# A two-layer attention and expert network on one core: a nineteenth weight slot in the second layer, and two more experts of the first layer added up in DRAM

## The chip, the core and the metric

The kernel runs on one core of a Trainium2 chip. The metric is the device time of one execution in microseconds (us), lower is better; a kernel is run several times and the median counts.

## What is computed

The reference is two layers over 512 latent tokens and 256 context tokens of width 1024, all in fp32. Each layer has three groups of mixing heads, an output projection, and then an expert-choice feed-forward: every one of 16 experts picks its own tokens (64 latent ones, and in the first layer 32 context ones), runs them through a gated two-matrix layer of width 512 and a down matrix, weighs the rows by the gate value and adds them back to their tokens. Cut to the part that matters here:

```python
def ec_ffn(h, router_w, w_gate, w_up, w_down):
    cap = EC_CAPACITY_FACTOR * n_tok // N_EXPERTS
    aff = jax.nn.softmax((h @ router_w).astype(jnp.float32), axis=-1)
    top_aff, idx = lax.top_k(jnp.swapaxes(aff, 1, 2), cap)
    xg = jax.vmap(lambda hb, ib: hb[ib])(h, idx)
    hid = jax.nn.silu(einsum(xg, w_gate)) * einsum(xg, w_up)
    y = einsum(hid, w_down) * top_aff[..., None]
    return zeros.at[idx].add(y)
...
xl = xl + g2 * ec_ffn(...)          # latent tokens, both layers
xc = xc + cg2 * ec_ffn(...)         # context tokens, first layer only
```

The result is the RMS-normed latent stream after the second layer.

## The kernel before, in words

`layer(li, ada)` is run for both layers; `upd` is true in the first one only. The last stage of a layer is a loop over the experts, `for e in range(NE + 1)`, and all of the change lies there and in the buffers that feed it. TensorE (PE) executes in the order in which the program is written (`manual_schedule`); the order on the other engines and on the DMA queues is set by the framework's scheduler, under the waits that tiles impose.

**Weights.** An expert has six halves of 1 MB: two of the gate matrix, two of the up matrix (`load_gu`), two of the down matrix (`load_d`). Each goes into a slot of 8 KB a partition. The slots come from several pools that `slot()` takes in a cycle: three of `ringa`, three or nine of `ringb` (`RING_B`), and `RING_D` more, opened once the output projection's operands are gone. In the second layer that makes 3 + 9 + 6 = 18 slots. The loads are issued on SP's queue (two in the second layer on POOL's), and each waits until PE has read the former content of its slot, and also, as SP's loads share eight semaphores in turn, until the load eight before it has landed. SP handles its list strictly in order.

**One turn of the loop.** PE does the gate and up matmuls of expert e (`gate_up`: 64 rows, in the first layer also 32 context rows), the down matmuls of expert e - 1 for the latent rows (`down`, called by `finish`), the transposes of the gathered rows of expert e + 1 (`columns`, evacuated into `xgT` by ACT at L1013 and DVE at L1015), the transposes of the hidden rows (`hid_t`, evacuated into `hTe` by ACT at L1053), and some pieces of `combine`. In the first layer `hid_t` belongs to expert e itself and the down matmuls of the 32 context rows come at the end of the turn; in the second layer rows are gathered for two experts at once.

**Adding the rows back.** There are two ways. For experts below `in_dram` (12 in the first layer, 0 in the second) DVE scales the down result into a tile `ya` of 96 rows (L1073) and POOL adds its rows to `acc`, a copy of the stream in DRAM, with an indirect DMA that accumulates (L1076). For the others DVE scales it into `yt` (L1082), ACT and DVE split it into a high and a low part `yp` (L1086, L1087; the context rows go to `y1`, L1095, and later to `yc`), POOL builds a one-hot matrix `pl`, and PE multiplies the two (`combine`, tile `cb`) so that DVE can add the product to the stream `xl` or `xc` in SBUF (L1120). `combine` covers two experts at a time for the latent rows: 16 matmuls into eight pieces, each of which one DVE addition takes up. `todo` holds the pieces; `fill` emits some of them a turn and the rest after the loop. Before the first such addition the stream is read back from `acc`: six DMAs on POOL's queue (L1194), in turn NE - 2.

What follows after the loop in the first layer is the second layer's norm of `xl` (ACT, L307), which needs the last additions.

## Time and profile before

| | |
|---|---|
| runs of the kernel | 1432.83 us median (1432.7, 1432.83, 1435.84) |
| the profiled execution's own time | 1436.76 us |
| its span, first to last instruction | 1435.0 us |
| mean granted clock of TensorE | 0.958 |
| PE busy | 1284.1 us (89%) |
| DVE, ACT, POOL busy | 710.2, 513.5, 216.7 us |
| moved by DMA | 321.16 MB |
| experts of the first layer | about 520 to 840 us of the span |
| experts of the second layer | about 1190 to 1420 us |

A busy PE is not PE at its peak, since matmuls are pipelined and their ends are modelled. So the argument goes by stretches of the span: who waits for whom there, what the granted clock is, and how busy the DMA engines are.

### The profile page before, as it was taken

Reading aid. Unit: us, or ns where it says so; the run is one execution under the profiler, and the core shown is the slowest. Engines: PE = TensorE matmul, PEld = TensorE weight load, DVE = VectorE, ACT = ScalarE, POOL = GpSimd, SP = SyncE. Lnnn points to the kernel's source line nnn. Section 1 sums busy time; section 2 is a strip of 40 time slices with the busy share of each in tenths; the row PEclk is TensorE's granted clock in tenths of the full one; section 3 lists DMA queues with packets and bytes.
Section 4 is the critical chain, followed back from the end, with each engine's and each line's share of the span. In section 5 each row is a group of like instructions: output and inputs, shape, how many; then the busy total and the mean of one; then the engine's idle time right before and its main releaser. Section 6 shows DMA issues by size and latency. Waiting matters only on the chain. (4 is left out here: it accounts for less than half of the span.)

```text
span 1435.0 us, 21605 instructions
## 1 busy us (share of the span) xinstructions
PE 1284.1 (89%) x8598; PEld 811.0 (57%) x8598; DVE 710.2 (49%) x1564; ACT 513.5 (36%) x1093; POOL 216.7 (15%) x252
## 2 busy tenths in 40 slices
PE   3989989989999959999999959998999968999986
PEld 0768866656678833444443438876778754343332
DVE  1545266566653453333333484847876352333435
ACT  2523145455543322222222143436666232232222
POOL 1111001313120230111110120101232011111201
PEclk9989999999999979999999989999999988999998
DMA  9523416535661389999999610210016447999993
GB/s 359 190 88 118 161 40 235 184 132 195 246 235 54 138 313 363 374 375 376 374 374 389 243 57 32 72 63 1 2 35 258 163 190 303 419 420 419 420 421 124
DMA packets 54084, 321.16 MB, mean 224 GB/s; under 512 B 8528, under 2 KB 8656, under 8 KB 20448
## 3 DMA queue, kind: packets, MB, share of 16 engines
q1 hardware_dynamic: 45664, 286.75, 51.2%
q0 software_dynamic: 8320, 33.03, 7.2%
q8 instruction: 68, 1.11, 0.3%
q14 instruction: 32, 0.26, 0.1%
HBM read 304.52 MB, written 15.24 MB: 223 GB/s over the span
## 5 line engine op out<-in xcount | busy, mean ns | idle before, releaser
L59 PE MATMUL mm<-slot,xgT 128*32 128x256 f32 (+1 forms) x2048 | 289.1, 492 | 5.6 <-DMA slot<-in_exp_w_up_dram 3.9
L59 PE MATMUL mm<-hT,w 128*128 128x512 f32 (+1 forms) x1176 | 228.9, 354 | 3.3 <-POOL w L135 2.0
L59 PEld LDWEIGHTS mm<-hT,w 128*128 128x128 f32 x1176 | 191.4, 191 | 37.1 <-POOL w L135 2.4
L59 PEld LDWEIGHTS mm<-slot,xgT 128*32 128x32 f32 (+1 forms) x2048 | 104.2, 125 | 178.7 <-issue 144.7
L59 PE MATMUL mm<-slot,hTe 128*32 128x256 f32 (+1 forms) x1024 | 150.2, 503 | 0.8 <-ACT hTe L1053 0.8
L1044 DVE TENSOR_TENSOR gh<-mm,gh 64x512 f32<-64x512 f32 (+1 forms) x48 | 29.0, 604 | 226.7 <-ACT gh L1043 225.5
L1043 ACT ACTIVATE gh<-mm 64x512 f32<-64x512 f32 (+1 forms) x48 | 24.9, 519 | 243.1 <-PE mm L59 243.1
L59 PE MATMUL mm<-wo,mixb 128*128 128x512 f32 x360 | 99.1, 411 | 2.3 <-DVE mixb L135 1.3
L1013 ACT ACTIVATE xgT<-tp,modT,a 128x64 f32<-128x64 f32 (+1 forms) x192 | 68.9, 426 | 84.3 <-PE tp L1009 80.9
L59 PEld LDWEIGHTS mm<-slot,hTe 128*32 128x32 f32 (+1 forms) x1024 | 51.1, 126 | 81.5 <-issue 69.1
L689 ACT COPY pt<-tp 128x512 f32<-128x512 f32 (+1 forms) x120 | 64.9, 542 | 82.6 <-PE tp L686 81.4
L686 PE MATMUL tp<-ident,p 128*128 128x128 f32 x552 | 87.4, 284 | 5.5 <-ACT pt L689 2.3
L676 POOL TENSOR_SCALAR p<-p,sm 128x768 f32<-128x768 f32 (+1 forms) x30 | 58.5, 1950 | 124.4 <-DVE sm L675 116.1
L686 PEld LDWEIGHTS tp<-ident,p 128*128 128x128 f32 x552 | 61.5, 142 | 27.8 <-issue 18.7
L59 PE MATMUL ada<-slot,sT 128*32 128x512 f32 x384 | 54.6, 689 | 23.6 <-DMA slot<-in_ada_w_dram 23.6
L59 PEld LDWEIGHTS mm<-wo,mixb 128*128 128x128 f32 x360 | 65.3, 192 | 16.9 <-DVE mixb L135 2.2
L59 PE MATMUL sc<-kt,qh 96*128 96x512 f32 (+1 forms) x324 | 69.7, 348 | 0.0
L134 ACT CAST w<-slot 128x1024 fp32r<-128x1024 f32 x30 | 31.4, 1046 | 100.1 <-PE mm L59 73.8
L59 PE MATMUL sc<-kst,qst 128*128 128x256 f32 (+1 forms) x288 | 48.1, 298 | 20.6 <-DVE mx L673 12.9
L665 DVE TENSOR_REDUCE mx<-sc 128x1 f32<-128x768 f32 (+1 forms) x60 | 51.0, 851 | 26.9 <-PE sc L59 25.9
L996 POOL DMA_INDIRECT xg<-tabx,gidx x24 | 23.2, 968 | 252.4 <-PE tp L1051 149.4
L59 PEld LDWEIGHTS sc<-kt,qh 96*128 96x128 f32 x324 | 52.6, 190 | 10.0 <-issue 3.4
(246 smaller groups left out, 1794.6 us busy)
## 6 DMA issues: line engine op xcount, KB each, us to landing
slot<-in_exp_w_gate_dram SPq DMA_DIRECT2D x62, 1024.0 KB
slot<-in_exp_w_up_dram SPq DMA_DIRECT2D x62, 1024.0 KB
slot<-in_exp_w_down_dram SPq DMA_DIRECT2D x62, 1024.0 KB
slot<-in_ada_w_dram SPq DMA_DIRECT2D x48, 1024.0 KB
slot<-in_win_dram SPq DMA_DIRECT2D x14, 1024.0 KB
slot<-in_wo_dram SPq DMA_DIRECT2D x8, 1024.0 KB
tabx<-xn POOLq DMA_DIRECT2D x10, 512.0 KB, 3.0
xt<-in_x_dram SPq DMA_DIRECT2D x4, 512.0 KB
```

The lines of the kernel that those rows point to most:

```text
L59: PE.matmul(o, l, r, start=start, stop=stop, skip_group_check=True)
L134: (hi or V.tensor_copy)(out[0], x)
L665: V.tensor_reduce(mx, sc[:, :n], axis=AX.X, op=OP.max, negate=True)
L676: (G if s and self.kind == "mla" else V).tensor_scalar(p[:, :n], p[:, :n], sm, None, op0=OP.mult)
L686: PE.transpose(ps[:, b * 128:(b + 1) * 128], p[:, (b0 + b) * 128:(b0 + b + 1) * 128], ident)
L689: S.copy(o, ps[:, :n * 128])
L996: G.indirect_dma_start(out=xg, out_offset=None, in_=tabx[li], in_offset=bass.IndirectOffsetOnAxis(ap=gidx[:ng, c:c + 1], axis=0))
L1013: S.activation(xgT[:, k0 + k, :n], ps[:, k * ng:k * ng + n], AF.Identity, bias=b[:, 0:1], scale=s[:, 0:1])
L1043: S.activation(gh[64:128, :n], ps[0:64, :n], AF.Silu)
L1044: V.tensor_tensor(gh[0:64, :n], ps[64:128, :n], gh[64:128, :n], op=OP.mult)
```

## The change

`RING_D` gives the second layer seven slots instead of six there, 19 in all. The room is made in the pool `ex`: one `xgT` instead of two in both layers, and in the second layer one `gh` and one `hTe` instead of two. In the first layer `in_dram` rises from 12 to 14: experts 12 and 13 (they are counted from 0) are added up in `acc` as well, and only 14 and 15 go through `combine`. With that the read-back moves from the middle of turn 14 to its end, behind the accumulating DMA of expert 13, and the context tile `y1` holds rows of two experts only, so that `split` takes its upper 64 partitions.

```diff
--- before.py
+++ after.py
@@ -35,7 +35,7 @@
 RING_0 = 6
 RING_A = 3
 RING_B = (3, 9)
-RING_D = (8, 6)
+RING_D = (8, 7)
 AHEAD = 2
 PB = 5
 PTB = 3
@@ -1002,7 +1002,7 @@
                 xgTs[e] = xgTs[e - 1]
                 return
             xg = xgs[e]
-            xgT = xgTs[e] = ex.tile([128, KD, ng], F32, name="xgT")
+            xgT = xgTs[e] = ex.tile([128, KD, ng], F32, name="xgT", bufs=1)
             for k0 in range(0, KD, 4):
                 ps = ps_tp()
                 for k in range(4):
@@ -1039,7 +1039,7 @@
                     for q in range(4):
                         mm(ps[32 * q:32 * q + 32, :n], xgT[:, k, CAPL:],
                            wgu[q // 2][k][:, (q % 2) * n:(q % 2 + 1) * n], k == 0, k == KD - 1)
-            gh = hids[e, r] = ex.tile([128, FF], F32, name="gh")
+            gh = hids[e, r] = ex.tile([128, FF], F32, name="gh", bufs=2 if upd else 1)
             S.activation(gh[64:128, :n], ps[0:64, :n], AF.Silu)
             V.tensor_tensor(gh[0:64, :n], ps[64:128, :n], gh[64:128, :n], op=OP.mult)
 
@@ -1049,7 +1049,7 @@
             ps = ps_tp()
             for c in range(n // 128):
                 PE.transpose(ps[:, c * 64:c * 64 + 64], hid[0:64, c * 128:(c + 1) * 128], ident[:64, :64])
-            hT = hTs[e, r] = ex.tile([128, n // 2], F32, name=f"hTe{r}")
+            hT = hTs[e, r] = ex.tile([128, n // 2], F32, name=f"hTe{r}", bufs=2 if upd else 1)
             S.copy(hT, ps[:, :n // 2])
 
         Y = {}
@@ -1089,7 +1089,7 @@
                 return
 
             i = e % np_
-            if i == 0:
+            if e == in_dram:
                 Y[r] = ex.tile([128, D], F32, name=f"y{r}", bufs=1)
             for q in range(np_):
                 V.scalar_tensor_tensor(Y[r][i * rows:(i + 1) * rows, q * n:(q + 1) * n], ps[rows * q:rows * (q + 1), :n],
@@ -1105,9 +1105,9 @@
 
         def split(g):
 
-            o = [ex.tile([128, D], F32R, name=f"yc{i}", bufs=1) for i in range(2)]
-            parts(Y[1], o, S.copy)
-            pl = places(1, g)
+            o = [ex.tile([128, D], F32R, name=f"yc{i}", bufs=1)[64:128] for i in range(2)]
+            parts(Y[1][64:128], o, S.copy)
+            pl = places(1, g)[64:128]
             return [(pl, [y[:, hf * 512:(hf + 1) * 512] for hf in range(2)]) for y in o]
 
         def combine(r, terms):
@@ -1126,7 +1126,7 @@
         rs = range(len(streams))
         todo, pair = [], []
 
-        in_dram = 12 if upd else 0
+        in_dram = NE - 2 if upd else 0
 
         def finish(e, r):
             down(e, r)
@@ -1148,7 +1148,7 @@
                 x = X["xl"][tb]
                 for hf in range(2):
                     steps[2 * tb + hf]()
-                    j = p.tile([128, 512], F32, name="gh")
+                    j = p.tile([128, 512], F32, name="gh", bufs=1)
                     S.activation(j, x[:, hf * 512:(hf + 1) * 512], AF.Square, accum_out=sq2[:, tb, hf:hf + 1])
                 sq = small.tile([128, 1], F32, name="ssq")
                 V.tensor_tensor(sq, sq2[:, tb, 0:1], sq2[:, tb, 1:2], op=OP.add)
@@ -1187,11 +1187,6 @@
                     columns(e + 1)
                 if e + 2 < NE:
                     gather(e + 2)
-                if upd and e == NE - 2:
-
-                    for i, t in enumerate(X["xl"] + X["xc"]):
-                        V.tensor_copy(t[:, 0:1], xgTs[NE - 1][:, 0, 0:1])
-                        G.dma_start(t, acc[i * 128:(i + 1) * 128, :])
                 if upd:
                     for r in reversed(rs):
                         hid_t(e, r)
@@ -1199,6 +1194,11 @@
             if e:
                 for r in rs[1:] if upd else rs:
                     finish(e - 1, r)
+            if upd and e == in_dram:
+
+                for i, t in enumerate(X["xl"] + X["xc"]):
+                    V.tensor_copy(t[:, 0:1], xgTs[NE - 1][:, 0, 0:1])
+                    G.dma_start(t, acc[i * 128:(i + 1) * 128, :])
         if upd:
             fill(len(todo))
         else:
```

PE's list loses the 16 `cb` matmuls of experts 12 and 13 and is otherwise the same. On the engines and queues that the prediction speaks of, the order moves as follows.

ACT in turn 13 of the first layer (`xgT` and `hTe` are the evacuations that PE's transposes wait for, `yp` is the split of expert 12), before:

```order
L1013 ACTIVATE xgT<-tp,modT_102,a_0_2041 128x64 x2
L1086 CAST yp<-yt 64x512 x2
L1013 ACTIVATE xgT<-tp,modT_102,a_0_2041 128x64 x2
L1053 COPY hTe_6729<-tp 128x128
L1013 ACTIVATE xgT<-tp,modT_102,a_0_2041 128x64 x2
L1053 COPY hTe_6736<-tp 128x256
L1013 ACTIVATE xgT<-tp,modT_102,a_0_2041 128x64 x2
```

and in the change:

```order
L1043 ACTIVATE gh<-mm 64x256
L1043 ACTIVATE gh<-mm 64x512
L1013 ACTIVATE xgT<-tp,modT_102,a_0_2041 128x64 x2
L1053 COPY hTe_6723<-tp 128x128
L1053 COPY hTe_6730<-tp 128x256
L1013 ACTIVATE xgT<-tp,modT_102,a_0_2041 128x64 x6
```

The two casts of `yp` are gone from between the evacuations, and `hTe` is no longer behind further pieces of `xgT`; turn 14 changes in the same way. This is also how turns 1 to 12 stand before and after.

POOL at the end of the first layer's experts, with the semaphores that each row waits for (DMASW are those of POOL's own DMAs), before:

```order
L1076 DMA acc<-ya,gidx 768x1024 [waits DMASW0_49,DVE_49]
L996 DMA xg<-tabx_88,gidx 96x1024 [waits DMASW1_49,PE_49]
L1194 DMA xl_3838<-acc 128x1024 [waits DMASW2_49,DVE_49]
L1194 DMA xl_3839<-acc 128x1024 [waits DVE_49]
L1194 DMA xl_3840<-acc 128x1024 [waits DVE_49]
L1194 DMA xl_3841<-acc 128x1024 [waits DVE_49]
L1194 DMA xc_3845<-acc 128x1024 [waits DVE_49]
L1194 DMA xc_3846<-acc 128x1024 [waits DVE_49]
L1103 TENSOR_SCALAR pl_6994<-tok,st_4662 128x512 [waits PE_49,Pool_49]
L1103 TENSOR_SCALAR pl_7069<-tok,st_4662 128x512 [waits PE_49,Pool_49]
```

and in the change:

```order
L996 DMA xg<-tabx_88,gidx 96x1024 [waits DMASW1_49,PE_49]
L1076 DMA acc<-ya,gidx 768x1024 [waits DMASW2_49,DVE_49]
L1076 DMA acc<-ya,gidx 768x1024 [waits DMASW4_49,DVE_49]
L1201 DMA xl_3838<-acc 128x1024 [waits DMASW5_49]
L1201 DMA xl_3839<-acc 128x1024
L1201 DMA xl_3840<-acc 128x1024
L1201 DMA xl_3841<-acc 128x1024
L1201 DMA xc_3845<-acc 128x1024
L1201 DMA xc_3846<-acc 128x1024 [waits DMASW3_49]
```

Two accumulating DMAs stand ahead of the read-back now, and its first DMA waits for the landing of the second of them. The one-hot matrices of experts 14 and 15 are built long before, in the place of those of 12 and 13.

SP in the second layer, the weight loads from the gate matrix of expert 12 on (each row is two halves, or as many as stand behind it), before (gate and up of 12; down of 11 and 12; gate and up of 13, of 14; down of 13; gate and up of 15; down of 14 and 15):

```order
L761 DMA slot<-in_exp_w_gate_dram 128x2048 x2
L761 DMA slot<-in_exp_w_up_dram 128x2048 x2
L769 DMA slot<-in_exp_w_down_dram 128x2048 x4
L761 DMA slot<-in_exp_w_gate_dram 128x2048 x2
L761 DMA slot<-in_exp_w_up_dram 128x2048 x2
L761 DMA slot<-in_exp_w_gate_dram 128x2048 x2
L761 DMA slot<-in_exp_w_up_dram 128x2048 x2
L769 DMA slot<-in_exp_w_down_dram 128x2048 x2
L761 DMA slot<-in_exp_w_gate_dram 128x2048 x2
L761 DMA slot<-in_exp_w_up_dram 128x2048 x2
L769 DMA slot<-in_exp_w_down_dram 128x2048 x4
```

and in the change (gate and up of 12, of 13; down of 12 and 13; gate and up of 14; one half of down of 14; gate and up of 15; the last three down halves):

```order
L761 DMA slot<-in_exp_w_gate_dram 128x2048 x2
L761 DMA slot<-in_exp_w_up_dram 128x2048 x2
L761 DMA slot<-in_exp_w_gate_dram 128x2048 x2
L761 DMA slot<-in_exp_w_up_dram 128x2048 x2
L769 DMA slot<-in_exp_w_down_dram 128x2048 x4
L761 DMA slot<-in_exp_w_gate_dram 128x2048 x2
L761 DMA slot<-in_exp_w_up_dram 128x2048 x2
L769 DMA slot<-in_exp_w_down_dram 128x2048
L761 DMA slot<-in_exp_w_gate_dram 128x2048 x2
L761 DMA slot<-in_exp_w_up_dram 128x2048 x2
L769 DMA slot<-in_exp_w_down_dram 128x2048 x3
```

Early down halves stand elsewhere in the stream now: ahead of expert 14's gate and up instead of ahead of expert 13's. And one half, of expert 3's gate matrix, has moved ahead of the point where SP first has to wait for PE to free a slot: counted from that point on SP's queue, the first half of the up matrix of expert 13 was the 63rd load and is the 60th; that of expert 14 was the 67th and is the 68th; the last load was the 78th and is the 77th.

## Rows read from the trace of the kernel before

**Rows 1.** PE in order of time, first layer, turns 12 to 14: start, length

```profile
738.49 10.76 PE L59 MATMUL mm<-slot,xgT 128*32 128x256 f32 x96
...
754.15 0.46 PE L1051 MATMUL tp<-ident,gh 64*128 64x64 f32 x4 [0.38 <-ACT hTe L1053]
754.53 1.93 PE L59 MATMUL mm<-slot,hTe 128*32 128x256 f32 x32
756.28 10.75 PE L59 MATMUL mm<-slot,xgT 128*32 128x256 f32 x96
...
773.80 0.69 PE L1051 MATMUL tp<-ident,gh 64*128 64x64 f32 x4 [2.26 <-ACT hTe L1053]
774.41 3.64 PE L59 MATMUL mm<-slot,hTe 128*32 128x256 f32 x32
```

**Rows 2.** Busy time by stretch: us, five engines (instructions), clock, DMA share, GB/s

```profile
760.00:800.00 40.00, 35.49 (x259) 14.85 (x260) 13.39 (x36) 10.49 (x28) 5.25 (x8) 0.88 0.98 378
```

**Rows 3.** PE in order of time, first layer, turn 15 and the end

```profile
799.80 10.94 PE L59 MATMUL mm<-slot,xgT 128*32 128x256 f32 x96
...
814.61 3.44 PE L59 MATMUL cb<-yp,pl 128*128 128x512 f32 x12
817.98 5.52 PE L59 MATMUL mm<-slot,hTe 128*32 128x256 f32 x48
...
830.53 5.50 PE L59 MATMUL cb<-yp,pl 128*128 128x512 f32 x15 [3.62 <-DVE yp L1087]
```

**Rows 4.** ACT in order of time there

```profile
824.42 1.26 ACT L1086 CAST yp<-yt 64x512 fp32r<-64x512 f32 x2 [9.33 <-PE cb L59]
```

**Rows 5.** DVE in order of time there, and its copies ahead of the read-back

```profile
814.22 0.75 DVE L1082 SCALAR_TENSOR_TENSOR yt<-mm,gw,g2l 128x512 f32<-128x512 f32 x1 [2.06 <-PE mm L59]
...
819.98 1.97 DVE L1095 SCALAR_TENSOR_TENSOR y<-mm,gw,g2c 32x256 f32<-32x256 f32 x4 [0.92 <-PE mm L59]
...
829.70 1.40 DVE L1087 TENSOR_TENSOR yp<-yt,yp 64x512 fp32r<-64x512 f32 x2
...
831.66 1.88 DVE L1120 TENSOR_TENSOR xl<-xl,cb 128x512 f32<-128x512 f32 x3
...
838.76 2.48 DVE L1120 TENSOR_TENSOR xc<-xc,cb 128x512 f32<-128x512 f32 x4 [0.59 <-PE cb L59]
...
L1193 DVE COPY xl<-xgT x4: 144/144/145, 794.1 to 794.5; 128x1 f32<-128x1 f32 x4
```

**Rows 6.** POOL in order of time: the accumulating DMA of expert 11

```profile
759.61 1.44 POOL L1076 DMA_INDIRECT acc<-ya,gidx  x1 [4.91 <-DVE ya L1073]
```

**Rows 7.** DMA issues by line, whole span: count, KB each, median us to landing

```profile
xl<-acc POOLq DMA_DIRECT2D x4, 512.0 KB, 7.6
...
xc<-acc POOLq DMA_DIRECT2D x2, 512.0 KB, 14.0
...
xg<-tabx,gidx POOLq DMA_INDIRECT x24, 9.3
acc<-ya,gidx POOLq DMA_INDIRECT x12, 9.8
```

**Rows 8.** PE in order of time, second layer, gate and up of experts 10, 12 to 14

```profile
1321.58 7.04 PE L59 MATMUL mm<-slot,xgT 128*64 128x512 f32 x32
...
1348.80 7.04 PE L59 MATMUL mm<-slot,xgT 128*64 128x512 f32 x32
...
1367.60 8.45 PE L59 MATMUL mm<-slot,xgT 128*64 128x512 f32 x30 [3.90 <-DMA slot<-in_exp_w_up_dram]
...
1382.85 7.04 PE L59 MATMUL mm<-slot,xgT 128*64 128x512 f32 x32
```

**Rows 9.** Busy time by stretch, second layer (columns as in rows 2)

```profile
1190.00:1205.00 15.00, 14.48 (x75) 7.78 (x75) 0.69 (x1) 4.78 (x10) 5.16 (x4) 0.90 0.55 186
1355.00:1370.00 15.00, 10.62 (x40) 3.68 (x38) 5.29 (x8) 2.20 (x4) 3.13 (x2) 0.90 1.01 420
```

**Rows 10.** The chain that ended last, its first piece: start, us, what

```profile
1189.91 4.32 DMA xg<-tabx,gidx
```

## The prediction

> **What bounds the kernel now.** I read the stretches that the change touches, not the shares over the span. In the first layer's experts a turn of PE's loop takes 17.79 us (738.49 to 756.28 [rows 1]), and within it PE waits 0.38 us for an evacuation by ACT. Turn 13 is different. Expert 12 is the first that isn't added up in DRAM; ACT makes its two `yp` casts between the evacuations, and PE waits 2.26 us for `hTe` instead of 0.38. The 32 matmuls after that wait took 3.64 us instead of 1.93: TensorE was granted its lower level, 1.2 of 2.4 GHz, after the wait, and over 760 to 800 us the mean is 0.88 [rows 1, 2]. Turn 14 repeats this, so turn 15 begins at 799.80 [rows 3], where two more turns of 17.79 us after 756.28 would have begun it at 791.86. Behind turn 15 stand the 16 `cb` matmuls of experts 12 and 13, then a wait of 3.62 us before the `cb` of 14 and 15 [rows 3]. The reason is in ACT's row: the cast of expert 14's `yp` had waited 9.33 us for PE to finish reading the `yp` of experts 12 and 13 [rows 4]. So the end of the first layer is a chain through ACT and DVE that begins with those two experts. DMA isn't late there: no row of PE in it waits for one.
>
> In the second layer PE and DMA run neck and neck. The DMA engines are full (share 1.01, 420 GB/s [rows 9]), so a half of 1.05 MB takes 2.5 us, and PE catches up with the stream once: in turn 13 it waits 3.90 us for the first up half of expert 13 and then takes 8.45 us for 30 matmuls, for which the row at full clock gives 30/32 of 7.04, or 6.60 [rows 8]; the clock's mean over 1355 to 1370 us is 0.90, its lower level again [rows 9].
>
> **The change, part by part.**
>
> *First layer, turns 13 and 14.* The `yp` casts leave ACT's list, so these turns become like turn 12, and turn 15 begins at 756.28 + 2 x 17.79 = 791.86. In turn 14 DVE's six one-column copies remain; at 0.145 us each they may hold up an evacuation, and I add all six, 0.87 [rows 5]: 792.73 instead of 799.80. (Bounds: 0 to 0.87 for the copies.) DVE's work for an expert becomes six `ya` scalings in place of `yt`, `yp` and `y1`; this is what turns 1 to 12 carry within 17.79 us.
>
> *First layer, the end.* From the start of turn 15 to the end of its transposes nothing changes: 814.61 - 799.80 = 14.81 us [rows 3]. That gives 807.54. No `cb` follows; PE does the 48 down matmuls in 5.52 us at once [rows 3]: 813.06. The `yp` of expert 14 is made beside them, since its buffers are free. Expert 15: `yt` 0.75, the first cast on ACT 0.63 (half of 1.26), then two subtractions of 0.70, which hide the second cast: 815.84; then four pieces of `y1`, 1.97: 817.81 [rows 4, 5]. There DVE's additions to `xl` begin. Before, they began at 831.66 [rows 5], and from there to the second layer the work is the same (eight additions, the context's part, the norm). **Term: -13.85 us.** In it are the two long waits, the low clock, the 16 `cb` matmuls (4.6 us at 3.44 for twelve) and the wait behind them; I don't add them again.
>
> *The read-back, now late.* The accumulating DMA of expert 11 was issued 3.33 us after turn 13 began (759.61 against 756.28 [rows 1, 6]), so that of expert 13 comes at 792.73 + 3.33 = 796.06 and lands 9.8 us later, at 805.9 [rows 7]. The six loads follow at once, some 0.56 us apart. In the trace they took 7.6 us (`xl`) and 14.0 us (`xc`), beside a full stream of weights [rows 7]. So `xl` is there at about 813.5 and the last `xc` at 808.7 + 14.0 = 822.7. They are needed at 817.8, and, as the additions to `xc` began 7.1 us after those to `xl` [rows 5], at 824.9. I cost the read-back at nothing; the cover is 4.3 and 2.2 us, and what exceeds it is paid in full. The trace of before shows no wait of this kind, since the last accumulating DMA was issued at 759.61 and the copies ahead of the read-back ran at 794.1 [rows 5, 6]. The Trainium skill, page "DMA: Bandwidth & Descriptors", section "Two DMAs through the same engine are not ordered", says that a DMA which reads what an earlier one writes is ordered by nothing but the earlier one's completion semaphore, even on one queue. By that rule the loads cannot be queued behind the accumulating DMA at 797.5 and must start at 805.9; the sum stays as it is by either, and only the chance of the first rival rises.
>
> *Two more accumulating DMAs* put 0.4 MB each into a busy stretch, about 1 us of the engines each at 420 GB/s; PE waits for no DMA there, so nothing.
>
> *One buffer for `xgT`, `gh`, `hTe`.* On PE the readers of the old content stand ahead of the transposes or matmuls whose result replaces it, or (for `gh`) directly behind, with a whole turn until it is needed: nothing. If that fails, an evacuation would be late by one group of transposes, under 1 us a turn.
>
> *Second layer, the nineteenth slot.* One half more is loaded before PE begins, so each later place in the stream is worth 2.5 us less, and the order has changed. Expert 13's first up half was the 63rd load and landed at about 1367.6; as the 60th it lands at 1360.1, before PE asks for it: that wait goes. Next is expert 14's, the 68th: 1367.6 + 5 x 2.5 = 1380.1. PE needs two turns of together 27.22 us from turn 12 on (1348.80 - 1321.58 [rows 8]) and is there at 1376.0. So it waits 4.1 us one turn later. If it then runs as slowly as before, for 8.45 - 6.60 = 1.85 us, turn 14 counts as begun at 1381.95 instead of 1382.85 [rows 8]. **Term: -0.9 us** (bounds: -2.75 without the slow start, +1 if the stream restarts less smoothly, a rounding of half a load).
>
> *Second layer, the first gather.* The extra half joins the burst of loads that ends about when the gather of the first two experts is issued: between 1190 and 1205 us the engines are at 0.55 [rows 9], and the gather took 4.32 us [rows 10]. Beside a full stream a gather takes 9.3 us [rows 7]. With 2.5 us more of load in front it lies between +0 and +5.0; only part of one half can still be ahead of it, so I take half of 2.5. **Term: +1.3 us**, on the path, as PE's first matmuls wait for it and the stream's restart waits for PE.
>
> **Sum:** -13.85 - 0.9 + 1.3 = -13.45 us. The profiled execution took 1436.76 us, 1.76 above its span of 1435.0; it would take 1423.3. The median of the runs, 1432.83, is 3.9 below that execution, and I take the difference over: **1419.4 us**.
>
> **The rivals.** *The read-back is late.* For: it has to wait for a landing that nothing made it wait for before, and its cover is 2 to 4 us. Against: the durations I used are those beside a full stream, while the last weights are in by then. It decides from a landing of the accumulating DMA at 808.1 on. With loads of twice the length, `xl` would come at 821.1 (3.3 us late) and `xc` at 836.7 (11.8 late): 1422.7 to 1431.2.
>
> *The second layer's wait goes for good and the gather isn't delayed.* Then 3.90 + 1.85 us and the small remainder vanish: 1432.83 - 13.85 - 5.75 = 1413.2. For: PE has only this one long wait there [rows 8]. Against: DMA is the fuller of the two [rows 9], and expert 14's halves are five places later.
>
> *Slower than before.* The six loads run one after the other instead of side by side, behind the wait. At 7.6 us each the last is in at 805.9 + 45.6 = 851.5, which is 26.6 us after it is needed: 1446. It decides from 5.4 us for one load on, (824.9 + 13.45 - 805.9) / 6. Against: issued 0.56 us apart, the sixth took 14.0 us, so together they needed about 2.8 us each even then.
>
> *The change doesn't do what it says:* the slot frees no earlier load, the first layer's part holds: 1420.3 or, with the gather, 1420; this lies within the forecast's range.
>
> **How the numbers follow.** Forecast (1416 to 1422.5): 0.72. Late read-back: 0.13. Second layer wins fully: 0.09. Slower: 0.03. No change, because another chain stands right behind the first layer's end: 0.03. A measurement of this kernel can tell about 0.3%, 4.3 us, from no change. Forecast, the second layer's win and most of the late read-backs are faster by more: 0.93; 0.03 for the same (the rest of the late ones, and most of no change), 0.04 slower (the slower rival, and what is left of no change). The range from 1413.5 to 1425 leaves out half of the late read-backs, a part of the second layer's win, and the last two: under 2 in 10.
>
> **What would show it.** Right: PE's waits for `hTe` in turns 13 and 14 about 0.4 us and the clock 1.00 over 760 to 800; turn 15 at about 792.7; the read-back issued near 806; the first addition to `xl` near 818, after DVE's `y1`; in the second layer no DMA wait in turn 13 and one of about 4 us in turn 14; a wait of 1 to 2 us for the first gather. Wrong: DVE's or PE's first `cb` row waiting for the `xl` load, or the layers' border less than 10 us earlier.

## The result, and the profile after

The changed kernel takes 1422.2 us (median of 8 runs, 1417.35 to 1427.99); the kernel before, run beside it, 1436.16 us (8 runs). The ratio is 0.9901, 95% interval [0.9877, 0.9925]: about 1% faster, inside the range and 2.8 us above the number given. The profiled execution of the change took 1423.59 us; the working, made against the profiled execution of before, had given 1423.3.

Cut at marks that both profiles have (starts of PE's rows), the two executions compare so:

| stretch | before, us | after, us | predicted | measured |
|---|---|---|---|---|
| start to turn 0 of the first layer's experts | 528.23 | 525.71 | 0 | -2.52 |
| turn 0 to turn 15 | 271.57 | 265.05 | -7.07 | -6.52 |
| turn 15 to the second layer's first transposes | 45.09 | 38.90 | -6.78 | -6.19 |
| from there to the transposes behind the router's choice | 343.41 | 346.34 | 0 | +2.93 |
| from there to gate and up of expert 0 | 7.25 | 7.95 | +1.3 | +0.70 |
| from there to the end | 239.44 | 237.87 | -0.9 | -1.57 |
| sum (span) | 1434.99 | 1421.81 | -13.45 | -13.18 |

The two predicted parts of the first layer are the term of 13.85, split at the start of turn 15. The rows with +2.93 and -2.52 hold only work that the change leaves alone; over the fourteen profiles of this study the fourth one lies between 341.1 and 346.4 us, at a mean clock between 0.95 and 0.92. That the sums agree to 0.3 us is partly luck: these two rows nearly cancel, and in the four others the first layer gave 1.14 us less than forecast and the second 1.27 us more.

PE in order of time, first layer, turns 13 to 15 and the end of the layer:

```profile
755.17 10.75 PE L59 MATMUL mm<-slot,xgT 128*32 128x256 f32 x96
...
770.82 0.46 PE L1051 MATMUL tp<-ident,gh 64*128 64x64 f32 x4 [0.39 <-ACT hTe L1053]
771.21 1.93 PE L59 MATMUL mm<-slot,hTe 128*32 128x256 f32 x32
772.96 10.76 PE L59 MATMUL mm<-slot,xgT 128*32 128x256 f32 x96
...
790.76 10.75 PE L59 MATMUL mm<-slot,xgT 128*32 128x256 f32 x96
...
805.39 7.38 PE L59 MATMUL mm<-slot,hTe 128*32 128x256 f32 x80
812.70 2.12 PE L59 MATMUL cb<-yp,pl 128*128 128x512 f32 x6
816.58 4.23 PE L59 MATMUL cb<-yp,pl 128*128 128x512 f32 x10 [1.76 <-DVE xl L1120]
```

Against [rows 1, 3]: the wait for `hTe` in turn 13 is 0.39 us and no longer 2.26, the 32 matmuls behind it take 1.93 us and no longer 3.64, and turns 13 and 14 last 17.79 and 17.80 us. The 16 `cb` matmuls between the down matmuls are gone.

DVE in order of time at the end of the layer (answers to [rows 5]):

```profile
807.87 1.97 DVE L1095 SCALAR_TENSOR_TENSOR y<-mm,gw,g2c 32x256 f32<-32x256 f32 x4
810.96 0.75 DVE L1082 SCALAR_TENSOR_TENSOR yt<-mm,gw,g2l 128x512 f32<-128x512 f32 x1 [1.12 <-PE mm L59]
812.40 1.40 DVE L1087 TENSOR_TENSOR yp<-yt,yp 64x512 fp32r<-64x512 f32 x2 [0.69 <-ACT yp L1086]
813.83 1.98 DVE L1095 SCALAR_TENSOR_TENSOR y<-mm,gw,g2c 32x256 f32<-32x256 f32 x4
815.84 3.13 DVE L1120 TENSOR_TENSOR xl<-xl,cb 128x512 f32<-128x512 f32 x5
```

The additions to `xl` begin 815.84 - 790.76 = 25.08 us after turn 15, and the working had 817.81 - 792.73 = 25.08. No addition waits for a load. POOL's rows say why:

```profile
794.08 1.42 POOL L1076 DMA_INDIRECT acc<-ya,gidx  x1 [16.36 <-DVE ya L1073]
803.76 2.26 POOL L1201 DMA_DIRECT2D xl<-acc  x4 [8.26 <-DMA acc<-ya,gidx]
805.97 1.10 POOL L1201 DMA_DIRECT2D xc<-acc  x2
```

The accumulating DMA of expert 13 is issued 3.32 us after turn 15 begins, POOL waits 8.26 us for it to land, and the four loads of `xl` land 5.0 to 7.2 us after their issues (the first at 808.8, the last at 812.6), those of `xc` 8.0 and 10.1 us after (the last at 816.6). DVE comes to `xl` at 815.84 and to `xc` at 823.38.

PE in the second layer, turns 12 to 14 (answers to [rows 8]):

```profile
1336.21 1.02 PE L59 MATMUL mm<-slot,xgT 128*64 128x512 f32 x2
1340.24 8.45 PE L59 MATMUL mm<-slot,xgT 128*64 128x512 f32 x30 [3.00 <-DMA slot<-in_exp_w_up_dram]
...
1354.67 7.04 PE L59 MATMUL mm<-slot,xgT 128*64 128x512 f32 x32
...
1368.51 1.02 PE L59 MATMUL mm<-slot,xgT 128*64 128x512 f32 x2
1370.11 7.08 PE L59 MATMUL mm<-slot,xgT 128*64 128x512 f32 x30 [0.58 <-DMA slot<-in_exp_w_up_dram]
```

The wait for weights has gone from turn 13, and stands as 3.00 us in turn 12, with the slow 8.45 us behind it, and as 0.58 us in turn 14. Busy time by stretch (answers to [rows 2, 9]) shows a granted clock of 1.00 in the first layer's stretch, where it was 0.88, and of 0.88 around turn 12. The middle row begins 5.5 us before gate and up of expert 0, as the stretch from 1190 us did before; the DMA engines are at 0.64 there and were at 0.55:

```profile
760.00:800.00 40.00, 39.22 (x338) 16.42 (x336) 13.93 (x38) 8.48 (x24) 3.79 (x3) 1.00 1.02 384
1178.40:1193.40 15.00, 13.09 (x72) 6.41 (x72) 0.69 (x1) 4.78 (x10) 4.38 (x4) 0.97 0.64 224
1336.00:1350.00 14.00, 11.00 (x42) 3.85 (x40) 2.34 (x4) 2.03 (x4) 0.00 (x0) 0.88 1.02 420
```

The first gather of the second layer heads the chain that ended last, and takes 5.09 us instead of 4.32 [rows 10]; PE waits 1.79 us for it:

```profile
1177.55 5.09 DMA xg<-tabx,gidx
```

### The profile page after: what moved, and what is told of

Its sections match the earlier page's. It is cut to its first block, busy times and chain, and to the rows that moved or that the text cites. A ratio compares the mean times of both kernels' runs of the same rounds, so it can differ in the third digit from the quotient of the medians.

```text
span 1421.8 us, 21561 instructions
## 1 busy us (share of the span) xinstructions
PE 1278.7 (90%) x8582; PEld 809.6 (57%) x8582; DVE 704.3 (50%) x1554; ACT 512.0 (36%) x1089; POOL 216.4 (15%) x252
## 5 line engine op out<-in xcount | busy, mean ns | idle before, releaser
L59 PE MATMUL mm<-slot,hTe 128*32 128x256 f32 (+1 forms) x1024 | 147.0, 489 | 1.2 <-ACT hTe L1053 1.1
L1120 DVE TENSOR_TENSOR xl<-xl,cb 128x512 f32<-128x512 f32 x72 | 45.8, 683 | 44.4 <-PE cb L59 43.4
```

Source lines behind the costliest of these rows:

```text
L59: PE.matmul(o, l, r, start=start, stop=stop, skip_group_check=True)
L1120: V.tensor_tensor(x, x, ps, op=OP.add)
```

## The experiments

Kernels that ran together are compared with the same runs of the kernel before, on their chip. Some verdicts lean on the time, others on a stretch of the trace, since a difference of 2 or 3 us is within the interval of most ratios here.

**1. The first layer's part alone** (`RING_D` and the buffers as before, everything else of the change in).

> The first layer's part alone: fourteen experts added up in DRAM and the read-back at the end of turn 14, with 18 slots and the old buffers. My theory (nearly all of the gain is made between turn 13 and the layers' border): faster by 13 to 15 us; the additions to xl begin about 14.7 us earlier than before once the drift at turn 12 is taken off; in the second layer PE waits some 4 us in turn 13 as before, and from its first gate and up matmul to the end it takes 239.5 us as before. Rival (the second layer carries a good part): faster by 10 us or less, and the additions to xl come early but some wait behind them takes the time back.

Measured: ratio 0.9909 [0.9877, 0.9942], 1424.9 against 1437.45 us, 12.6 faster. Turn 0 to 15 takes 263.79 us, turn 15 to the norm's transposes 38.58, gate and up of expert 0 to the end 240.80, with the wait of 3.92 us in turn 13 as before. So the first layer carries the gain; the rival falls.

**2. The second layer's part alone** (19 slots and the single buffers, twelve experts in DRAM).

> The second layer's part alone: 19 slots and the single buffers, twelve experts in DRAM as before. My theory (the slot only moves the wait for weights): within 0.3% of before, at most 2 us faster; first layer as before; PE waits about 3 us for up weights in turn 12 and under 1 us in turn 14, none in turn 13, and the first gather costs it 1 to 2 us. Rival (the slot is worth the whole wait): about 5.7 us faster, no wait for weights. Rival (the slot delays the gather for nothing): 1 to 2 us slower.

Measured: 0.9978 [0.9954, 1.0002], 1436.23 us; the last stretch takes 239.43 us against 239.44 of before. PE waits 2.67 us in turn 12 and 1.93 in turn 14, the slow row (8.78 us) stands behind the second; the gather's stretch is 7.44 us:

```profile
1352.10 7.08 PE L59 MATMUL mm<-slot,xgT 128*64 128x512 f32 x30 [2.67 <-DMA slot<-in_exp_w_up_dram]
...
1381.97 8.78 PE L59 MATMUL mm<-slot,xgT 128*64 128x512 f32 x30 [1.93 <-DMA slot<-in_exp_w_up_dram]
```

The slot moves the wait and takes little from it. Over all profiles with the loads in the old order the last stretch is 237.87 to 239.43 us with 19 slots (four profiles) and 239.44 to 241.29 with 18 (six), 2.1 us apart in the mean.

This run's first layer, which has the casts of before, shows something else: turn 0 to 15 takes 268.92 us, 2.65 less than before. The wait for `hTe` in turn 13 is 2.26 us as before, but the row behind it isn't slow, at a granted clock of 1.00 (776 to 788 us); in turn 14 the row behind the same wait is slow again (3.19 us). So the slow row doesn't follow that wait every time.

```profile
775.61 0.46 PE L1051 MATMUL tp<-ident,gh 64*128 64x64 f32 x4 [2.26 <-ACT hTe L1053]
776.00 1.93 PE L59 MATMUL mm<-slot,hTe 128*32 128x256 f32 x32
```

**3. The single buffers without the slot.**

> The single buffers for xgT, gh and hTe without the slot they make room for (18 slots, twelve experts in DRAM). Theory one (a single gh reorders DVE, so that PE's short waits for an addition in the even turns go, 0.35 us in two turns, but the weights are the bound in turn 13): two turns take 26.87 us in place of 27.22, PE comes some 2 us earlier to turn 13 and waits 5.5 to 6 us there in place of 3.9; total within 1 us of before. Theory two (PE is the bound): 2 us faster. Theory three (single buffers cost something): two turns take longer than 27.22 us and the total is 1 us or more slower.

Measured: 1.0005 [0.9985, 1.0024]. PE, second layer, turns 10, 12 and 13:

```profile
1323.03 7.04 PE L59 MATMUL mm<-slot,xgT 128*64 128x512 f32 x32
...
1349.90 7.04 PE L59 MATMUL mm<-slot,xgT 128*64 128x512 f32 x32
...
1364.81 1.04 PE L59 MATMUL mm<-slot,xgT 128*64 128x512 f32 x2 [1.72 <-DMA slot<-in_exp_w_gate_dram]
1369.71 8.47 PE L59 MATMUL mm<-slot,xgT 128*64 128x512 f32 x30 [3.86 <-DMA slot<-in_exp_w_up_dram]
```

Two turns take 26.87 us and not 27.22, and the two waits together are 5.58 us, where before had 3.90 [rows 8] and a first one of 0.24: theory one. No cost of the single buffers shows; PE's gain ends in the wait for weights.

**4. The change, with the loads in the order in which PE reads them.** Nothing else is touched; the queue then holds gate and up of expert 12, down of 11, gate and up of 13, down of 12, and so on.

```diff
-        @early(-30)
+        @early(-30 if upd else 10)
         def load_gu(e, q=Q):
-            wgu = wgus[e] = []
-            for w in ("exp_w_gate", "exp_w_up"):
-                ws = []
-                for k in range(0, KD, 4):
+            wgu = wgus[e] = [[], []]
+            for k in range(0, KD, 4):
+                for ws, w in zip(wgu, ("exp_w_gate", "exp_w_up")):
                     t = slot([128, 4, FF])
...
```

> The change with the second layer's weight loads in the order in which PE reads them: gate and up of an expert ahead of the down of the one before, and gate and up halves in turn. Theory one (the wait left in the second layer is a matter of order, since down halves of 11 and 13 are loaded some 10 us before PE wants them, and the second gate half ahead of the first up half): PE waits for no weights in turns 12 to 15, the slow start behind the wait goes, and the kernel is about 5 us faster than the change, 1417 us beside 1436 of before, ratio 0.9865. Theory two (DMA is the bound whatever the order): the wait comes back in turn 14 or 15 or ahead of a down matmul, and the time is that of the change, ratio 0.990.

Measured: 0.9832 [0.9803, 0.9862], 1415.33 us; this interval lies below that of the change. In the trace the last stretch is 232.08 us against the change's 237.87, 5.8 less, and one short wait for weights is left, with no slow row behind it:

```profile
1376.70 4.46 PE L59 MATMUL mm<-slot,xgT 128*64 128x512 f32 x18
1381.39 3.65 PE L59 MATMUL mm<-slot,xgT 128*64 128x512 f32 x14 [0.24 <-DMA slot<-in_exp_w_up_dram]
```

Theory one holds, but for that wait of 0.24 us. What bound the change there was the order and not the rate of the DMA engines: the wait was for halves that stood behind others which PE did not want yet.

**5. The same with 18 slots** (`RING_D = (8, 6)`, the single buffers stay).

> The change and the demand order of the loads, but with 18 slots (the single buffers stay). In the run with 19 slots PE waited for weights once, 0.24 us, for the second up half of expert 15, and that of expert 14 had landed 0.9 us ahead of need. Theory one (in the right order the slot is one half of lead, 2.5 us): PE waits some 1.7 us in turn 14 and 1 to 2.5 us in turn 15, with a slow stretch behind one of them: from the first gate and up matmul to the end 235 to 237 us in place of 232.05, and the time is 2.5 to 5 us above that of the 19 slots. Theory two (order alone did it, the slot is worth nothing): 232 to 233 us and the same time.

Measured: 0.9839 [0.9803, 0.9874], 1414.66 us: by time no difference from experiment 4, though an interval of 10 us can't exclude 3. The last stretch takes 235.45 us, 3.4 more than with 19 slots. PE in turns 13 to 15:

```profile
1341.06 7.85 PE L59 MATMUL mm<-slot,xgT 128*64 128x512 f32 x32
...
1355.72 8.11 PE L59 MATMUL mm<-slot,xgT 128*64 128x512 f32 x32
...
1375.11 3.65 PE L59 MATMUL mm<-slot,xgT 128*64 128x512 f32 x14 [0.85 <-DMA slot<-in_exp_w_up_dram]
...
1393.38 5.49 PE L59 MATMUL cb<-yp,pl 128*128 128x512 f32 x15 [1.88 <-DVE yp L1085]
```

Turns 13 and 14 are longer by 0.81 and 1.07 us at a granted clock of 1.00, the wait of turn 15 by 0.61. The other 0.9 lies behind the start of the last row, which takes 5.49 us against 4.54; experiments 11 and 12 have the same slow row with 19 slots, so it isn't the slot's. So in the right order the slot gives some 2.5 us in this stretch, the size that theory one had, though the loss stands in longer rows and not in the waits that it named. What lengthens those rows is not shown, nor is the gain in the time.

**6. The kernel before with four buffers for `yp`** (`bufs=4 if upd else 3`).

> The kernel before with four buffers for yp in the first layer, nothing else. It takes away one wait of the old end of the layer: expert 14's cast for PE to finish reading the yp of 12 and 13 (9.33 us on ACT, 3.62 us on PE behind it). My theory (the end is a chain, this wait is a part of it, and the 16 cb matmuls, the casts between the evacuations and the low clock stay): the wait of 9.33 us goes, PE's of 3.62 us shrinks to under 1 us, the second round of additions to xl begins 3.5 to 5 us earlier, total 3 to 5 us faster. Rival (the yp buffers are what bounds the end): 8 us or more. Rival (DVE has the additions of 12 and 13 to do anyway and comes no earlier): under 1 us.

Measured: 0.9999 [0.9973, 1.0025]. The wait of 9.33 us is gone, and hardly anything is gained: the second round of additions begins 31.21 us after turn 15 (833.92 - 802.71), before it was 31.86. ACT's cast of expert 14, and DVE in order of time:

```profile
817.96 1.26 ACT L1086 CAST yp<-yt 64x512 fp32r<-64x512 f32 x2
```

```profile
818.34 0.69 DVE L1120 TENSOR_TENSOR xl<-xl,cb 128x512 f32<-128x512 f32 x1 [0.41 <-PE cb L59]
819.05 1.40 DVE L1087 TENSOR_TENSOR yp<-yt,yp 64x512 fp32r<-64x512 f32 x2
820.49 3.08 DVE L1120 TENSOR_TENSOR xl<-xl,cb 128x512 f32<-128x512 f32 x5
...
828.06 0.75 DVE L1082 SCALAR_TENSOR_TENSOR yt<-mm,gw,g2l 128x512 f32<-128x512 f32 x1 [1.59 <-PE mm L59]
...
833.92 4.87 DVE L1120 TENSOR_TENSOR xl<-xl,cb 128x512 f32<-128x512 f32 x8
```

DVE has the eight additions of experts 12 and 13 to do here, and PE its 16 `cb` matmuls; with those in the list the buffers are worth 0.65 us in the trace and nothing that shows in the time. The last rival was right, my theory wrong.

**7. The casts of experts 12 and 13 on GpSimd**, and **9. on DVE**, in the kernel before:

```diff
-                    S.copy(y[own, q], t[own])
+                    (G.tensor_copy if upd and e < NE - 2 else S.copy)(y[own, q], t[own])
```

> The kernel before with the yp casts of experts 12 and 13 on GpSimd in place of ACT, nothing else. Theory one (the casts stand between the evacuations, make PE wait 2.26 us for hTe, and the low clock follows that wait): hTe waits of turns 13 and 14 under 1 us, no low clock there, turn 15 begins 5 to 7 us earlier, and the total is 5 to 7 us faster; the wait of 9.33 us for the yp buffers stays. Rival (the casts on ACT cost nothing by themselves, the turn is slow because of DVE's share of the split): turn 15 begins within 1.5 us of before, total same.

> The kernel before with the yp casts of experts 12 and 13 on DVE in place of ACT, nothing else. On GpSimd they freed turn 13 but brought a new wait in turn 14, as the second of them stood behind a transfer; on DVE nothing of that kind can stand between. Theory one (the casts on ACT cost the two slow turns): hTe waits of turns 13 and 14 at most 1 us, the 32 matmuls behind them 1.93 us, turn 15 begins 263.5 to 265.5 us after turn 0 in place of 271.57, the stretch from turn 15 to the norm's first transposes stays at 45 us, total 6 to 8 us faster. Rival (any split beside the evacuations costs that, on whichever engine): turn 15 begins 269 us or more after turn 0, total within 3 us.

On GpSimd: 1.0016 [0.9993, 1.004]. Turn 13 becomes a turn like the others (17.79 us, `hTe` wait 0.39), but the second cast of turn 13 stands behind a gather on POOL, DVE's subtraction waits for it, and PE stands 6.41 us for `xgT` in turn 14; turn 15 begins 272.55 us after turn 0. It showed the mechanism for one turn and blurred the sum, hence the second version. On DVE both turns are freed. PE, turns 13 to 15:

```profile
770.01 0.46 PE L1051 MATMUL tp<-ident,gh 64*128 64x64 f32 x4 [0.39 <-ACT hTe L1053]
770.40 1.93 PE L59 MATMUL mm<-slot,hTe 128*32 128x256 f32 x32
772.15 1.73 PE L59 MATMUL mm<-slot,xgT 128*32 128x256 f32 x24
774.36 9.38 PE L59 MATMUL mm<-slot,xgT 128*32 128x256 f32 x72 [0.48 <-DVE xgT L1015]
...
790.78 1.71 PE L59 MATMUL mm<-slot,xgT 128*32 128x256 f32 x24
```

Turn 15 begins 264.46 us after turn 0, 7.1 earlier than before, and the clock over 760 to 800 us is 1.00: theory one, in the trace. The time does not follow: the ratio is 0.9987 [0.9963, 1.0011], median 1434.77 of 10 runs from 1425.36 to 1438.75; the profiled one, 1431.14, is below their median. Even the end of the interval, 5.3 us, is short of what was expected. In the profile 2.5 us of the 7.1 are given back, 0.7 at the end of the layer (45.77 us) and 1.85 in the last stretch (241.29 us). Where the rest goes in the other runs stays open.

**8. The read-back later still** (in the change, the copies ahead of it read DVE's last piece of `y1`, not `xgT`).

```diff
-            if upd and e == in_dram:
+        if upd:
...
-                    V.tensor_copy(t[:, 0:1], xgTs[NE - 1][:, 0, 0:1])
+                V.tensor_copy(t[96:128, 0:1], Y[1][96:128, 0:1])
```

> The change with the read-back issued later still, behind DVE's last piece of y1 (815.8 us in the profile of the change) and not behind turn 14: some 12.3 us later. It measures the cover. My theory (xl landed 3.2 us and xc 6.8 us ahead of need in the change, and what exceeds the cover is paid in full): the loads are issued at 816, xl lands from 821.3 on, the last xc at 829.0, DVE's last addition ends some 4.4 us later than in the change; total 4 to 6 us slower than the change. Rival (the read-back was the bound already, or it runs slower together with what stands there): 10 us or more slower. Rival (another chain to the second layer stands right behind): under 2 us.

Measured: 1424.17 us, 0.9899 [0.9856, 0.9941]. The loads are issued 25.4 us after turn 15 begins, 12.4 later than in the change, and now DVE waits for them:

```profile
814.83 1.22 DVE L135 TENSOR_TENSOR yc<-y,yc 64x1024 fp32r<-64x1024 f32 x1 [0.72 <-ACT yc L134]
818.02 2.69 DVE L1120 TENSOR_TENSOR xl<-xl,cb 128x512 f32<-128x512 f32 x4 [1.97 <-DMA xl<-acc]
```

From turn 15 to the norm's transposes it takes 43.08 us, 4.2 more than in the change (theory: 4.4). The ratio, beside 0.9901 of the change, doesn't show it: 4 us are within its interval. So by the trace the cover of the read-back was 12.4 - 4.2 = 8.2 us, with DVE's 1.2 us for `yc` moved ahead to fill part of it.

**10. Fifteen experts in DRAM** (`in_dram = NE - 1`).

> One step further than the change: fifteen experts in DRAM, the read-back behind the accumulating DMA of expert 14; only expert 15 goes through the one-hot matrices (a clearing of the unused 32 rows of y1 is added, off the path). My theory (the read-back is hidden up to fourteen and not beyond): the accumulating DMA of expert 14 is issued some 19 us after turn 15 begins and lands 28.5 us after, xl from 33 us and the last xc some 41 us after; from turn 15 to the norm's first transposes 45 to 47 us in place of 38.9, so 6 to 8 us slower than the change, 7 us faster than before. Rival (less work for DVE makes up for it): 38 to 40 us, the time of the change.

Measured: 0.9931 [0.9909, 0.9953], 1426.04 us, against 0.9901 of the change. From turn 15 to the norm 42.18 us, 3.3 more than the change, where 6 to 8 were expected. DVE, and POOL ahead of it:

```profile
820.71 1.28 DVE L1121 TENSOR_TENSOR xl<-xl,cb 128x512 f32<-128x512 f32 x2 [3.37 <-DMA xl<-acc]
```

```profile
811.17 1.40 POOL L1076 DMA_INDIRECT acc<-ya,gidx  x1 [14.13 <-DVE ya L1073]
816.94 2.26 POOL L1202 DMA_DIRECT2D xl<-acc  x4 [4.36 <-DMA acc<-ya,gidx]
```

The direction is that of my theory, by the trace; the intervals of the two ratios overlap. Fourteen is where the read-back still hides. The price was too high: with little beside it (68 GB/s over 811 to 817 us) the last accumulating DMA let POOL go on after 5.8 us (816.94 - 811.17) and not 9.5, so the read-back was issued 24.6 us after turn 15 began and not 28.5.

**11. The demand order without the turn of gate and up halves** (only `@early(-30 if upd else 10)`).

> The change with gate and up of an expert ahead of the down of the one before, but both gate halves ahead of the up halves as the change has them; it takes the two parts of the demand order apart. With halves in turn the first up half of expert 14 landed 2.2 us and that of 15 some 0.3 us ahead of need; here they come one load, 2.5 us, later. Theory one (both parts are needed): PE waits under 0.5 us in turn 14 and about 2 us in turn 15 for the first up half, perhaps with a slow stretch of 1.9 us behind it: 234 to 236 us from the first gate and up matmul to the end, between 232.08 and 237.87. Theory two (the place of the down halves is all): 232 to 232.5 us.

Measured: 0.9866 [0.9841, 0.9891], 1415.59 us. The last stretch takes 233.26 us, between the two theories; PE waits 0.83 us in turn 15 for the first up half. The place of the down halves gives 4.6 of the 5.8 us, the order within gate and up the other 1.2.

**12. The demand order, with the first two weight blocks of the second layer split on DVE** (`win(i, G if upd else V)`).

> The demand order (19 slots), and at the start of the second layer the low parts of the first two weight blocks are made by DVE and not by GpSimd. In all profiles the first two norm products xt of DVE take 2.84 us and the others 0.75 us, and just these two stand beside GpSimd's subtractions of 2.33 us. Theory one (the two engines slow each other): xt takes 0.75 us in all four, DVE does two subtractions of 1.22 us more, and from turn 15 to the first matmul on hT it is 1.7 us less, total some 1.7 us faster than the demand order alone, 1413.5 us. Theory two (the first two xt are slow for another reason): they stay at 2.84 us and DVE is 2.4 us later, total 1 to 2.4 us slower.

Measured: 0.9859 [0.9835, 0.9883], 1414.37 us. By time that is experiment 4 again; the stretch from turn 15 to the norm's transposes is 37.17 us against 39.43, and to the first matmul on `hT` 47.30 (837.87 - 790.57) against 49.37 (842.03 - 792.66), where the change has 48.84. DVE of experiment 12:

```profile
826.93 0.75 DVE L309 TENSOR_SCALAR xt<-xl,rs_r 128x1024 f32<-128x1024 f32 x1 [0.69 <-POOL rs_r L142]
827.60 1.22 DVE L135 TENSOR_TENSOR w<-slot,w 128x1024 fp32r<-128x1024 f32 x1
```

Theory one: `xt` takes 0.75 us when GpSimd has no subtraction beside it. The gain of 1.5 to 2.1 us is one of the trace alone.

Experiments 4, 5, 11 and 12 are all faster than the kernel before. The intervals of 4 and 5 lie below that of the change; those of 11 and 12 overlap it at 0.988, and there the last stretch decides (233.26 and 232.44 us against 237.87). Between the four the time decides nothing. Experiment 4 has the shortest last stretch and the lowest ratio, and is the version I would keep, with the split of experiment 12.

## Why the prediction was right, point by point

- *First layer, turns 13 and 14.* Right: they became turns of 17.79 us, and experiment 9 shows that the casts between ACT's evacuations had caused the wait and, with it, the slow row, which doesn't follow the wait every time (experiment 2). That the time of experiment 9 doesn't show the gain stays open. The six copies, costed at 0.87 us, cost nothing: turns 12 to 14 take 53.38 us, three times 17.79. That term was mis-sized by 0.87. Turn 0 to 15 still gained 6.52 us and not 7.94, since turn 0 itself ran its 96 matmuls in 13.14 us here and in 11.73 in the profile of before. That belongs to this one execution: in the seven other profiles with this first layer (experiments 1, 4, 5, 8, 10, 11, 12) turn 0 to 15 takes 263.56 to 263.79 us, 7.8 to 8.0 less than before.
- *First layer, the end.* The size was right up to the additions, 25.08 us in both; to the last digit that is luck, as the pieces are off by up to 0.2 us (the transposes end 14.63 us after turn 15 and not 14.81) and cancel. From the additions to the second layer, held to be the same as before, it took 13.82 us and not 13.23. The sentence on what bounds it was only half right: the cast's wait of 9.33 us is a link of the chain, but not one that can be taken out alone (experiment 6). What is left to pay is the work that goes, 16 matmuls on PE and eight additions on DVE; no run takes away these alone.
- *The read-back* cost nothing, as said. Its cover was put at 4.3 and 2.2 us; the dose of experiment 8 shows 8.2. The loads of 7.6 and 14.0 us that I took from [rows 7] had run beside a full stream; here they took 5.0 to 10.1. The program does what the rule asks that the prediction cited here (the Trainium skill, page "DMA: Bandwidth & Descriptors", section "Two DMAs through the same engine are not ordered": the first DMA's completion has to be waited for): POOL stands 8.26 us for that landing before it issues a load. No run leaves this wait out, so none shows that it is needed. The late read-back was the right rival to fear, and comes true one expert further on (experiment 10).
- *The nineteenth slot.* The wait did go from turn 13, as said, but it came back in another place: "no DMA wait in turn 13 and one of about 4 us in turn 14". I followed the halves of experts 13 and 14 along the stream and not those of 12. The first up half of 12 had been the 55th load and is the 56th; it lands at 1340.19, and PE asks for it at 1337.2. So the step that failed is the demand table: it has to hold every half, and PE's own pace after the change. A full table would not have been enough. At the prediction's rate (the 63rd load at 1367.6, 2.5 us a place) the 56th comes at 1350.1 on the time of before, and PE is due at 1349.8: a wait of 0.3 us and not 3.0. Counted from gate and up of expert 0, PE, which no longer loses 0.35 us in two turns, came 1.0 us earlier than before, and the half landed 1.7 us later than that rate gives. Why the stream was later is not shown. That the size came near (-1.57 in the profile against -0.9) is luck: the first up half of expert 14, the last one that PE waits for, let it go on 186.2 us after gate and up of expert 0, where the working gives 184.6, but no slow row stood behind it (7.08 us), for which 1.85 us had been put down; the two errors nearly cancel.
- *The gather* was late by 0.70 us, not 1.3. In the seven profiles with 19 slots its stretch takes 7.42 to 8.23 us, in the seven with 18 slots 7.22 to 7.33.
- *No gain of PE's own* had been costed for the single buffers. There is one: without the short waits for an addition two turns take 26.87 us. It is worth something only where weights don't follow behind (experiments 3 and 4).
- *Two slips in the working.* The wait of 4.1 us in turn 14 was counted from the start of the turn, but PE first does two matmuls with the gate half (1.02 us in the change), with which it would have been 3.1. And the rival in which the slot frees no earlier load comes to 1420.3 with the gather and to 1419.0 without it, not to 1420.3 and 1420; all of these lie in the range.
- *The base.* The 2.8 us between forecast and median come from the 3.9 us that I took off for the median of three runs. Over eight runs before has its median at 1436.16, next to the profiled execution.

## What to carry to other kernels

One more slot moves a wait along the stream; before adding one, write down for every load when it lands and when it is asked for, and see whether a load that isn't wanted yet stands ahead of one that is. Here a change of order on one queue was worth 5.8 us in a stretch from which the slot with its single buffers took 1.6 in the same profile. And a wait that stands in a chain is no measure of what its removal gives: give the waiting instruction its buffer and see whether the work behind it has anywhere to go.

## What the runs showed of the hardware

- *DVE beside GpSimd.* In the change, DVE's `xt` takes 2.84 us where GpSimd's subtraction of 2.33 us begins at the same time, and 0.75 us in the next blocks:

```profile
826.76 2.84 DVE L309 TENSOR_SCALAR xt<-xl,rs_r 128x1024 f32<-128x1024 f32 x1 [0.69 <-POOL rs_r L142]
...
833.89 0.75 DVE L309 TENSOR_SCALAR xt<-xl,rs_r 128x1024 f32<-128x1024 f32 x1 [0.67 <-POOL rs_r L142]
```

```profile
826.72 2.33 POOL L135 TENSOR_TENSOR w<-slot,w 128x1024 fp32r<-128x1024 f32 x1
```

  DVE's instruction ends 0.55 us after GpSimd's, as if it did most of its 0.75 us of work behind it. All thirteen profiles that have the subtraction on GpSimd show the two long `xt`; experiment 12 takes it away and the 2.09 us go. The Trainium skill, page "Trainium Architecture — The Big Picture", section "What this means for kernel authors", says that DVE and GpSimd share a port pair of SBUF under an exclusive lock; the trace agrees, with 2.84 us beside GpSimd and 0.75 us without.

- *An accumulating DMA* of 96 rows of 4 KB lets POOL go on 9.7 us after its issue beside the weight stream (803.76 - 794.08; 364 GB/s over 794 to 804 us), and 5.8 us after it with little beside it (experiment 10; 68 GB/s).

- *The spread of the runs goes with the granted clock.* The eight runs of the change go from 1417.35 us at a mean clock of 0.962 to 1427.99 us at 0.953, 10.6 us for 0.009. That is more than most edits here are worth, which is why stretches of the trace, with their own clock beside them, decide where a ratio doesn't.
